# Mask products of a chunked recurrence: each head in its own row half of the array, without block diagonals

## The chip, the cores and the metric

The kernel runs on one core of a Trainium2 chip. The metric is the device time in microseconds (us). Two versions of the kernel are compared by the median of their runs; profiles are of one execution each. TensorE is the matrix engine, VectorE, ScalarE and GpSimd do the elementwise work, and SyncE issues most of the transfers. In the rows these are PE (matmuls) and PEld (TensorE's weight loads), DVE, ACT, POOL and SP.

## The reference, cut to what matters

The program is two layers on 256 tokens of width 2048, in fp32: the first of attention and a state space scan, the second of a short convolution and an RWKV-7 recurrence, each with its gated feed-forward part. The change lies in the recurrence of the second layer alone, which has 16 heads of 64 channels and runs over 16 meta tokens and then the 256 tokens:

```
def step(s, inp):                       # s: (heads, 64 values, 64 keys)
    r_t, w_t, k_t, v_t, a_t, b_t = inp
    sa = jnp.einsum('bhvk,bhk->bhv', s, a_t)
    s = s * w_t[:, :, None, :] + sa[..., None] * b_t[:, :, None, :] + v_t[..., None] * k_t[:, :, None, :]
    y_t = jnp.einsum('bhvk,bhk->bhv', s, r_t)
    return s, y_t
```

with a_t = -kk (the normalised key), b_t = kk times a rate, k_t another key, r_t the receptance and w_t a decay per channel.

## The kernel before, in words

The kernel does this step by chunks: one chunk of the 16 meta tokens (padded to 32) and four chunks of 64 tokens. Inside a chunk the dependence of each token on the earlier ones is written as masked products of decayed keys. For each head and chunk there are two of these mask products. The first multiplies the pair (b, k) with a; it is masked strictly and kept as AA (AAm for the meta chunk). The second multiplies the same pair (b, k) with r; it is masked with the diagonal and kept as RB. AA is solved by forward substitution on VectorE (`substitute`), and RB gives the outputs.

The channels lie on the 128 partitions, two heads to a block j: head e=0 on partitions 0 to 63, head e=1 on 64 to 127. There are eight blocks. The tile bk holds, for a block and a chunk, 64 columns of b and 64 of k; ar holds a and r; bkm and arm are their meta forms.

A matmul with bk as the stationary operand contracts over all 128 partitions, that is over both heads. To keep the heads apart, the kernel before writes the moving operand as a block diagonal: a tile with 64 columns for each head, filled with that head's a (or r) on its own 64 partitions and with zeros, set once, on the others. For AA these tiles are AD (two of them, by the parity of j) and ADm, filled by `spread` (L1032) with four ScalarE copies for each block. For RB it is RD (one tile for four blocks of a chunk), filled inside `products` (L1243) with two ScalarE copies. One call for a block and chunk then gives both heads: 128 columns of output, in 128 partitions (64 for b and 64 for k). Four such calls fill one PSUM bank, which VectorE multiplies with the mask into AA or RB.

`mixing(p2)` (L1038) makes AA for the blocks 2 p2 and 2 p2 + 1, all four chunks, and their meta product. `products(ci, g)` makes RB of chunk ci for four blocks. Both take their PSUM from `self.ps()`, the tag m, which has two banks; four banks belong to the gemms (`self.acc`) and two to the tag a. TensorE writes these in fp32; a call of `self.mm` (L99) with fp32 operands is two loads and two matmuls. The gemms take weights and activations as two parts, hi and lo, with three products for each.

What sets the order: while the gemms of the mixer run, `step()` after each gemm part (12 matmuls or so) calls the next piece of the recurrence, from a list of steps or from a list of due slots (`at(slot, f)`). `keys`, `key_norms` and `mixing` of the four pairs go in the gemms of the keys (`self.steps`), the last `mixing(3)` at slot 10 of the gemms after them, then `fetch`, which sends AA through DRAM to the layout of the substitution; the chunks with their `values`, `products`, `turn_keys`, `state_in`, `solve`, `state_out` and `outputs` go by slots later. The framework then orders the instructions of each engine by its own simulated times, with the program's order as the priority, and adds all semaphores. Each engine then runs its instructions in that fixed order.

Of the kernel before, what the change touches and what calls it, by code (L numbers as in the profile page):

```python
# [12 lines left out]
ALU = mybir.AluOpType  # L13
# [4 lines left out]
P = 128  # L18
# [24 lines left out]
class Net:  # L43
# [850 lines left out]
    def block2_mixer(self):  # L894
        nc, a = self.nc, self.a
        v = nc.vector
# [11 lines left out]
        ar = self.t(pp, [P, 8, 4, 2, 64], "ar")  # L908
        bk = self.t(pp, [P, 8, 4, 2, 64], "bk")
        arm = self.t(pp, [P, 8, 2, 32], "arm")  # L910
        bkm = self.t(pp, [P, 8, 2, 32], "bkm")
# [30 lines left out]
        avp = self.pool("avp", ctx=c1)  # L942
        AV = self.t(avp, [P, 8, TOK], "AV")
        ms64, ms32 = self.mask(avp, "ms64", 64, True), self.mask(avp, "ms32", 32, True)
# [15 lines left out]
        hs = [slice(0, 64), slice(64, 128)]  # L960
        flat2 = lambda ap: ap.rearrange("p b t -> p (b t)")
# [33 lines left out]
        def keys(p2):  # L995
            wk = wk_[0]
            for i in range(2):
                j = 2 * p2 + i
                av = AV[:, j, :]
                en = self.t(wk, [P, 17 + 4 * 65], "en")  # L1000
                enc = en[:, 17:].rearrange("p (c t) -> p c t", t=65)[:, :, 1:]
                nc.scalar.activation(en, EL[:, j, :], AF.Exp, scale=DECAY)
                nc.scalar.activation(EL[:, j, :], EL[:, j, :], AF.Exp, scale=-DECAY)
                k = kt.pop(j)
                rp = self.ps("a")
                for s, (o, n) in enumerate(SEG):
                    lt = nbs[p2][:n, s * 4 + 2 * i:s * 4 + 2 * i + 2, :].rearrange("p e k -> p (e k)")
                    self.tr(rp[:, o:o + n], lt)
                kk = self.t(wk, [P, TOK], "w", bufs=4)
                v.scalar_tensor_tensor(kk, k, self.vec("k_k_2", j), rp[:, :TOK], op0=ALU.mult, op1=ALU.mult)  # L1010
                b = self.t(wk, [P, TOK], "w", bufs=4)
                v.tensor_tensor(b, kk, av, op=ALU.mult)
                nc.scalar.activation(av, av, AF.Identity, scale=self.vec("k_a_2", j), bias=oka[:, j:j + 1])
                kp = KP[:, j, :]
                v.tensor_tensor(kp, av, k, op=ALU.mult)
                v.scalar_tensor_tensor(ar[:, j, :, 0, :], main(kk), -1.0, ELc[:, j, :, 0:64],
                                       op0=ALU.mult, op1=ALU.mult)
                v.scalar_tensor_tensor(arm[:, j, 0, 0:META], kk[:, 0:META], -1.0, EL[:, j, 0:META],
                                       op0=ALU.mult, op1=ALU.mult)
                for w, src in ((0, b), (1, kp)):  # L1020
                    v.tensor_tensor(bk[:, j, :, w, :], main(src), enc, op=ALU.mult)
                    v.tensor_tensor(bkm[:, j, w, 0:META], src[:, 0:META], en[:, 1:17], op=ALU.mult)
                spread(j)

        AD = [self.t(avp, [P, 4, 2, 64], f"AD{i}") for i in range(2)]
        ADm = self.t(avp, [P, 2, 2, 32], "ADm")
        for x in (*AD, ADm):
            nc.gpsimd.memset(x, 0.0)
        AAe = AA.rearrange("p c (e j) t -> p c e j t", e=2)
        AAme = AAm.rearrange("p (e j) t -> p j e t", e=2)  # L1030

        def spread(j):  # L1032

            for e in range(2):
                nc.scalar.copy(AD[j % 2][hs[e], :, e, :], ar[hs[e], j, :, 0, :])
                nc.scalar.copy(ADm[hs[e], j % 2, e, :], arm[hs[e], j, 0, :])

        def mixing(p2):  # L1038

            for i in range(2):  # L1040
                j = 2 * p2 + i
                ps = self.ps()
                for c in range(4):
                    self.mm(ps[:, c * P:(c + 1) * P], flat2(bk[:, j, c, :, :]), flat2(AD[i][:, c, :, :]))
                v.tensor_tensor(AAe[:, :, :, j, :], ps.rearrange("p (c e t) -> p c e t", c=4, t=64),
                                ms64.unsqueeze(1).unsqueeze(1).to_broadcast([P, 4, 2, 64]), op=ALU.mult)
            ps = self.ps()
            for i in range(2):
                self.mm(ps[:64, i * 64:(i + 1) * 64], flat2(bkm[:, 2 * p2 + i, :, :]), flat2(ADm[:, i, :, :]))
            v.tensor_tensor(AAme[:, 2 * p2:2 * p2 + 2], ps[:64, :P].rearrange("p (j e t) -> p j e t", j=2, t=32),  # L1050
                            ms32.unsqueeze(1).unsqueeze(1).to_broadcast([64, 2, 2, 32]), op=ALU.mult)

        ac = self.gemm(w_in, 0, KT, R0 + 3072, [96, 96], self.xs2, TOK)
        self.shifted(zp, twd, ac[0], 24, 96)
# [4 lines left out]
        for p2 in range(4):  # L1059
            ac = self.gemm(w_in, 0, KT, R0 + 1024 + p2 * 256, [P, P], self.xs2, TOK)  # L1060
            if not p2:
                cl.close()
                wk = wk_[0] = self.pool("rwk", bufs=2, ctx=c1)
            for i in range(2):
                j = 2 * p2 + i
                kt[j] = self.t(wk, [P, TOK], "k", bufs=4)
                self.shifted(zp, kt[j], ac[i], 8 + j)
            self.steps = [None, part(key_norms, p2), part(mixing, p2 - 1) if p2 else None, part(keys, p2)]
# [121 lines left out]
        st_ = {}  # L1190
# [6 lines left out]
        def chunk(ci):  # L1197
            k = Chunk()
            k.C = C = 32 if ci == 0 else 64
            k.n = META if ci == 0 else 64  # L1200
            c = k.c = ci - 1
            if ci == 0:
                k.bk = lambda j: flat2(bkm[:, j, :, :])
                k.ar = lambda j: flat2(arm[:, j, :, :])
                k.rr = lambda h, g: arm[h, 4 * g:4 * g + 4, 1, :]
                k.aa = lambda e, j: AAm[:, 8 * e + j, :]
                k.v = lambda j: V[:, j, 16:80]
                k.mi = mi32
            else:
                k.bk = lambda j: flat2(bk[:, j, c, :, :])  # L1210
                k.ar = lambda j: flat2(ar[:, j, c, :, :])
                k.rr = lambda h, g: ar[h, 4 * g:4 * g + 4, c, 1, :]
                k.aa = lambda e, j: AA[:, c, 8 * e + j, :]
                k.v = lambda j: V[:, j, c * 64:c * 64 + 128]
                k.mi = mi64
            return k

        ch = [chunk(ci) for ci in range(5)]

        def open_chunks():  # L1220
            c2.close()
            c5.close()
            cE.close()
            st_["cp"] = self.pool("cp", bufs=1, ctx=c3)
            st_["XQ"] = self.t(st_["cp"], [P, 8, 2, 64], "XQ")
            st_["SD"] = self.t(st_["cp"], [P, 8, 2, 64], "SD")
            st_["RD"] = self.t(st_["cp"], [P, 4, 2, 64], "RD")
            nc.gpsimd.memset(st_["SD"], 0.0)
            nc.gpsimd.memset(st_["RD"], 0.0)

        def values(ci):

# [10 lines left out]
        def products(ci, g):  # L1243

            k = ch[ci]
            C = k.C
            RD = st_["RD"]
            if not g:
                k.RB = self.t(st_["cp"], [2 * C, 8, 2, C], "RB")
            for e in range(2):  # L1250
                nc.scalar.copy(RD[hs[e], :, e, :C], k.rr(hs[e], g))
            ps = self.ps()
            for i in range(4):
                j = 4 * g + i
                rd = RD[:, i, :, :C]
                self.mm(ps[:2 * C, 2 * i * C:2 * (i + 1) * C], k.bk(j), flat2(rd) if C == 64 else rd)
            v.tensor_tensor(k.RB[:, 4 * g:4 * g + 4], ps[:2 * C, :8 * C].rearrange("p (j e t) -> p j e t", j=4, t=C),
                            k.mi.unsqueeze(1).unsqueeze(1).to_broadcast([2 * C, 4, 2, C]), op=ALU.mult)

        def turn_keys(ci):  # L1260

# [138 lines left out]
        ORDER = "v0 v1 v2 v3 b0 b1 r0 r1 r2 r3 g c0 h0 b2 c1 h1 b3 c2 h2 c3 h3"  # L1400
        at = self.at
        at(10, part(mixing, 3))
        at(10 + 2, fetch)
        s0, ds = 14, 4
# [10 lines left out]
        names = ORDER.split()  # L1415
        m0 = max(m0 + 6, 0, 8 * max(i + 1 for i, x in enumerate(names) if x[0] in 'vrg') + 2)
        at(m0, open_chunks)
        at(m0, part(values, 0))
        at(m0 + 1, part(products, 0, 0))
# [4 lines left out]
        for ci in range(5):  # L1424
            o = m0 + 3 + int(ci * dc)
            for x in seq.split():
                nm, off = x.split(':')
                f, d, last, args = dict(i=(state_in, 0, 5, 1), s=(solve, 0, 5, 1), v=(values, 1, 5, 0),
                                        t=(state_out, 0, 4, 1), y=(outputs, 0, 5, 0), p=(products, 1, 5, 1),
                                        k=(turn_keys, 1, 4, 0), r=(turn, 0, 5, 0))[nm[0]]  # L1430
# [17 lines left out]
        with ExitStack() as c4:  # L1448
# [63 lines left out]
            for m in LATE:  # L1512
                d = self.t(wk, [P, 258], "d")
                v.tensor_tensor(d, M[:, m, :], row, op=ALU.mult)
                h = self.H[:, m, 14:]
# [256 lines left out]
```

## Time and profile before

| | |
|---|---|
| median of 3 runs | 2443.42 us (2443.02 to 2444.26) |
| the profiled execution | 2443.2 us, of which the span from first to last instruction is 2441.4 us |
| TensorE, matmuls and loads | busy 99% and 96% |
| VectorE, ScalarE, GpSimd | busy 67%, 46%, 2% |
| granted TensorE clock, mean | 0.998 of full speed |
| HBM | 175 GB/s over the span |

Busy times are sums over the whole span, or over a stretch where one is named. Matmuls overlap one another, and the end of each is modelled, so a busy TensorE may still be slowed; the distance from the start of one weight load to the start of the next is the better measure of what an instruction costs. In a timeline, instructions that follow one another with the same line and tiles stand in one row with their number, and its duration is from the start of the first to the end of the last. Line 99 is the helper that records every matmul, line 104 every transpose, so groups are told apart by their tiles.

### The profile page before, as it was taken

To read this page: it belongs to the slowest core of one execution; us is meant where nothing else is said; L and a number is where in the kernel's file an instruction comes from. 1 tells how busy PE (TensorE), PEld (TensorE's weight loads), DVE (VectorE), ACT (ScalarE), POOL (GpSimd) and SP (SyncE) were. 2 spreads that over 40 slices of the span, in tenths; PEclk is the share of its full clock that TensorE was granted. 3 is DMA by queue.
4 is the path that set the end of the run, shared out by engine and by line. 5 is a ranking of instruction groups with operands and counts; after the bars stand their busy time and mean duration, and the time that the engine had idled before them with its cause. 6 is when DMAs were issued, how large, how long until landed. Compare 5 with 4: busy or idle time off the path is not lost.

```text
span 2441.4 us, 46809 instructions
## 1 busy us (share of the span) xinstructions
PE 2419.5 (99%) x19655; PEld 2347.5 (96%) x19655; DVE 1645.8 (67%) x2857; ACT 1131.4 (46%) x1574; POOL 59.4 (2%) x229
## 2 busy tenths in 40 slices
PE   9999999999999999999999999999999999999998
PEld 9999999999999999999999989999998999889986
DVE  7667666776676577567678956856865566556656
ACT  6545554443444344345664444454544444434443
POOL 3000000000000000000000000000000000000000
PEclk9999999999999999999999999999999999999999
DMA  7666446555655655656446551464555555555554
GB/s 226 178 186 164 155 156 200 181 185 182 198 183 174 197 190 173 197 183 209 148 138 190 167 148 53 139 210 155 192 190 189 184 181 188 190 188 181 185 190 138
DMA packets 402132, 431.09 MB, mean 177 GB/s; under 512 B 18849, under 2 KB 375780, under 8 KB 401456
## 3 DMA queue, kind: packets, MB, share of 16 engines
q1 hardware_dynamic: 386912, 413.41, 52.8%
q10 hardware_dynamic: 13184, 12.04, 1.7%
q0 software_dynamic: 1824, 2.64, 1.0%
q8 instruction: 154, 2.52, 0.4%
q14 instruction: 58, 0.48, 0.1%
HBM read 421.83 MB, written 6.23 MB: 175 GB/s over the span
## 4 chain that ended last, share of the span: by engine, by line
PE 97%; DVE 1%; issue 0%; DMA 0%; ACTq 0%; ACT 0%; SPq 0%; DVEq 0%
PE acc L99 89%; PE a L99 4%; PE m L99 3%; PE m L104 1%; PE a L104 1%; DVE lo L109 0%; DMA raw<-in_w_in_dram 0%; DVE sub L1106 0%; ACTq L1122 0%; DVE sub L1107 0%; ACT hi L108 0%; DVE F L1732 0%; DVE KP L1352 0%; DVE hx L1389 0%; DVE sub L1115 0%
## 5 line engine op out<-in xcount | busy, mean ns | idle before, releaser
L109 DVE TENSOR_TENSOR lo<-raw,hi 128x1024 fp32r<-128x1024 f32 (+1 forms) x780 | 951.2, 1220 | 627.1 <-ACT hi L108 620.4
L108 ACT CAST hi<-raw 128x1024 fp32r<-128x1024 f32 (+1 forms) x780 | 815.6, 1046 | 1130.7 <-PE acc L99 1044.5
L99 PE MATMUL acc<-Xh,lo 128*128 128x256 f32 (+3 forms) x4296 | 1214.9, 283 | 3.5 <-DVE lo L109 3.5
L99 PE MATMUL acc<-Xh,hi 128*128 128x256 f32 (+3 forms) x4296 | 1213.9, 283 | 4.6 <-ACT Xh L115 2.4
L99 PE MATMUL acc<-Xl,hi 128*128 128x256 f32 (+3 forms) x4296 | 1216.9, 284 | 0.5 <-DVE Xl L116 0.5
L99 PEld LDWEIGHTS acc<-Xh,lo 128*128 128x128 f32 x4296 | 811.7, 189 | 6.2 <-DVE lo L109 4.6
L99 PEld LDWEIGHTS acc<-Xh,hi 128*128 128x128 f32 x4296 | 810.7, 189 | 7.2 <-ACT Xh L115 2.6
L99 PEld LDWEIGHTS acc<-Xl,hi 128*128 128x128 f32 x4296 | 808.2, 188 | 2.5 <-DVE Xl L116 0.9
L99 PE MATMUL acc<-ghi,lo 128*128 128x256 f32 x704 | 196.7, 280 | 0.4 <-DVE lo L109 0.4
L99 PE MATMUL acc<-glo,hi 128*128 128x256 f32 x704 | 196.8, 280 | 0.0
L99 PE MATMUL acc<-ghi,hi 128*128 128x256 f32 x704 | 196.7, 280 | 0.0
L99 PEld LDWEIGHTS acc<-ghi,lo 128*128 128x128 f32 x704 | 132.2, 188 | 0.7 <-DVE lo L109 0.7
L99 PEld LDWEIGHTS acc<-glo,hi 128*128 128x128 f32 x704 | 132.4, 188 | 0.0
L99 PEld LDWEIGHTS acc<-ghi,hi 128*128 128x128 f32 x704 | 132.3, 188 | 0.0
L99 PE MATMUL acc<-lo,ghi 128*128 128x512 f32 (+1 forms) x326 | 128.3, 394 | 0.0
L99 PE MATMUL acc<-hi,glo 128*128 128x512 f32 (+1 forms) x326 | 128.2, 394 | 0.0
L99 PE MATMUL acc<-hi,ghi 128*128 128x512 f32 (+1 forms) x326 | 116.1, 394 | 0.0
L99 PEld LDWEIGHTS acc<-hi,glo 128*128 128x128 f32 x326 | 61.1, 188 | 14.9
L99 PEld LDWEIGHTS acc<-hi,ghi 128*128 128x128 f32 x326 | 61.3, 188 | 14.4
L99 PEld LDWEIGHTS acc<-lo,ghi 128*128 128x128 f32 x326 | 61.1, 187 | 14.6
L817 DVE SCALAR_TENSOR_TENSOR fc<-fu,vt,fc 128x256 f32<-128x256 f32 x176 | 73.4, 480 | 0.0
L99 PE MATMUL acc<-M2l,hi 128*128 128x258 f32 x256 | 72.4, 285 | 0.5 <-DVE M2l L109 0.5
(492 smaller groups left out, 2304.7 us busy)
## 6 DMA issues: line engine op xcount, KB each, us to landing
raw<-in_w_in_dram SPq DMA_DIRECT2D x90, 1024.0 KB, 5.4
raw<-in_w_up_dram SPq DMA_DIRECT2D x88, 1024.0 KB, 5.2
raw<-in_w_gate_up_dram SPq DMA_DIRECT2D x87, 1024.0 KB, 5.2
raw<-in_w_down_dram SPq DMA_DIRECT2D x76, 1024.0 KB, 5.2
raw<-in_w_out_dram SPq DMA_DIRECT2D x32, 1024.0 KB, 5.5
raw<-in_w_down_dram SPq DMA_DIRECT2D x24, 512.0 KB, 3.4
Hd<-H ACTq DMA_DIRECT2D x1, 2176.0 KB, 10.0
H<-Hd ACTq DMA_DIRECT2D x1, 2176.0 KB, 9.4
```

What stands on the lines that cost most here:

```text
L99: self.nc.tensor.matmul(out, lhsT, rhs, start=start, stop=stop, skip_group_check=True)
L104: self.nc.tensor.transpose(out, in_, self.ident[base:base + p, base:base + p])
L108: self.nc.scalar.copy(hi, src)
L109: self.nc.vector.tensor_sub(lo, src, hi.bitcast(F32))
L817: v.scalar_tensor_tensor(c, u[:, tp:tp + SEQ], self.vec(f"ffn_conv_w:{tp}", m), c, op0=ALU.mult, op1=ALU.add)
```

## The change

The block diagonals AD, ADm and RD, their clearing and their copies go. Each head multiplies with its own 64 partitions of bk and of ar alone (`h` in `hs` is 0:64 or 64:128), so that a call has 64 rows of contraction, 128 columns of bk (64 for the meta chunk) and the 64 (32) columns of one head. The two heads of a block write to two PSUM banks, `two[0]` and `two[1]`, and each bank is masked by one VectorE instruction. `mixing` now fills both banks with eight calls of each head (two blocks, four chunks) before it masks them; `products` with four calls of each head. The two heads' calls alternate.

```diff
-                spread(j)
-        AD = [self.t(avp, [P, 4, 2, 64], f"AD{i}") for i in range(2)]
-        ADm = self.t(avp, [P, 2, 2, 32], "ADm")
-        def spread(j):
-            for e in range(2):
-                nc.scalar.copy(AD[j % 2][hs[e], :, e, :], ar[hs[e], j, :, 0, :])
-                nc.scalar.copy(ADm[hs[e], j % 2, e, :], arm[hs[e], j, 0, :])
         def mixing(p2):
+            two = [self.ps() for _ in range(2)]
             for i in range(2):
                 j = 2 * p2 + i
-                ps = self.ps()
                 for c in range(4):
-                    self.mm(ps[:, c * P:(c + 1) * P], flat2(bk[:, j, c, :, :]), flat2(AD[i][:, c, :, :]))
-                v.tensor_tensor(AAe[:, :, :, j, :], ps.rearrange("p (c e t) -> p c e t", c=4, t=64),
+                    for e, h in enumerate(hs):
+                        self.mm(two[e][:, (c * 2 + i) * 64:(c * 2 + i + 1) * 64], flat2(bk[h, j, c, :, :]),
+                                ar[h, j, c, 0, :])
+            for e in range(2):
+                v.tensor_tensor(AAe[:, :, e, 2 * p2:2 * p2 + 2, :], two[e].rearrange("p (c i t) -> p c i t", c=4, t=64),
                                 ms64.unsqueeze(1).unsqueeze(1).to_broadcast([P, 4, 2, 64]), op=ALU.mult)
-            ps = self.ps()
+            two = [self.ps() for _ in range(2)]
             for i in range(2):
-                self.mm(ps[:64, i * 64:(i + 1) * 64], flat2(bkm[:, 2 * p2 + i, :, :]), flat2(ADm[:, i, :, :]))
-            v.tensor_tensor(AAme[:, 2 * p2:2 * p2 + 2], ps[:64, :P].rearrange("p (j e t) -> p j e t", j=2, t=32),
-                            ms32.unsqueeze(1).unsqueeze(1).to_broadcast([64, 2, 2, 32]), op=ALU.mult)
+                for e, h in enumerate(hs):
+                    self.mm(two[e][:64, i * 32:(i + 1) * 32], flat2(bkm[h, 2 * p2 + i, :, :]), arm[h, 2 * p2 + i, 0, :])
+            for e in range(2):
+                v.tensor_tensor(AAme[:, 2 * p2:2 * p2 + 2, e, :], two[e][:64, :64].rearrange("p (j t) -> p j t", t=32),
+                                ms32.unsqueeze(1).to_broadcast([64, 2, 32]), op=ALU.mult)
...
-            st_["RD"] = self.t(st_["cp"], [P, 4, 2, 64], "RD")
-            nc.gpsimd.memset(st_["RD"], 0.0)
...
         def products(ci, g):
+            two = [self.ps() for _ in range(2)]
+            for i in range(4):
+                for e, h in enumerate(hs):
+                    self.mm(two[e][:2 * C, i * C:(i + 1) * C], k.bk(4 * g + i, h), k.rr(h, 4 * g + i))
             for e in range(2):
-                nc.scalar.copy(RD[hs[e], :, e, :C], k.rr(hs[e], g))
-            ps = self.ps()
-            for i in range(4):
-                j = 4 * g + i
-                rd = RD[:, i, :, :C]
-                self.mm(ps[:2 * C, 2 * i * C:2 * (i + 1) * C], k.bk(j), flat2(rd) if C == 64 else rd)
-            v.tensor_tensor(k.RB[:, 4 * g:4 * g + 4], ps[:2 * C, :8 * C].rearrange("p (j e t) -> p j e t", j=4, t=C),
-                            k.mi.unsqueeze(1).unsqueeze(1).to_broadcast([2 * C, 4, 2, C]), op=ALU.mult)
+                v.tensor_tensor(k.RB[:, 4 * g:4 * g + 4, e], two[e][:2 * C, :4 * C].rearrange("p (j t) -> p j t", t=C),
+                                k.mi.unsqueeze(1).to_broadcast([2 * C, 4, C]), op=ALU.mult)
```

## Rows read from the trace of the kernel before

**Rows 1.** The page, part 1: busy us (share of the span) xinstructions, by engine.
```profile
PE 2419.5 (99%) x19655; PEld 2347.5 (96%) x19655; DVE 1645.8 (67%) x2857; ACT 1131.4 (46%) x1574; POOL 59.4 (2%) x229
```

**Rows 2.** The page, part 4: the chain that ended last, by engine.
```profile
PE 97%; DVE 1%; issue 0%; DMA 0%; ACTq 0%; ACT 0%; SPq 0%; DVEq 0%
```

**Rows 3.** Two stretches: busy us (instructions) of PE, PEld, DVE, ACT, POOL; clock, DMA.
```profile
1215.00:1300.00 85.00, 85.00 (x682) 82.52 (x682) 66.21 (x173) 50.80 (x96) 2.59 (x16) 1.00 0.48 145
...
1440.00:1550.00 110.00, 110.00 (x1209) 101.69 (x1207) 74.62 (x169) 54.96 (x90) 6.03 (x7) 1.00 0.23 68
```

**Rows 4.** The tile AD: duration in ns min/median/max, first and last start.
```profile
L99 PEld LDWEIGHTS m<-AD,bk x64: 186/192/193, 1222.5 to 1293.6; 128*128 128x128 f32 x64
...
L1035 ACT COPY AD<-ar x16: 388/402/404, 1218.5 to 1285.6; 64x256 f32<-64x256 f32 x16
```

**Rows 5.** The tile ADm, the same columns.
```profile
L1036 ACT COPY ADm<-arm x16: 214/216/221, 1219.3 to 1286.2; 64x32 f32<-64x32 f32 x16
L99 PEld LDWEIGHTS m<-ADm,bkm x16: 133/138/139, 1229.4 to 1295.0; 128*64 128x64 f32 x16
```

**Rows 6.** The tile RD, the same columns.
```profile
L99 PEld LDWEIGHTS m<-RD,bk x64: 186/192/193, 1459.5 to 1535.8; 128*128 128x128 f32 x64
...
L99 PEld LDWEIGHTS m<-RD,bkm x16: 132/138/139, 1446.2 to 1449.1; 128*64 128x64 f32 x16
...
L1251 ACT COPY RD<-ar x16: 401/404/407, 1449.5 to 1530.4; 64x256 f32<-64x256 f32 x16
L1251 ACT COPY RD<-arm x4: 295/297/299, 1442.3 to 1447.3; 64x128 f32<-64x128 f32 x4
```

**Rows 7.** Timeline of weight loads: start, us, form, number; a burst on RD.
```profile
1459.35 0.19 PEld L99 LDWEIGHTS acc<-Xh,lo 128*128 128x128 f32 x1
1459.47 0.97 PEld L99 LDWEIGHTS m<-RD,bk 128*128 128x128 f32 x8
1460.37 0.19 PEld L99 LDWEIGHTS acc<-Xh,hi 128*128 128x128 f32 x1
```

**Rows 8.** The same timeline: a burst of 64 rows by 64 columns.
```profile
1468.99 0.19 PEld L99 LDWEIGHTS acc<-Xh,hi 128*128 128x128 f32 x1
1469.32 1.94 PEld L99 LDWEIGHTS a<-XQ,AA 64*64 64x64 f32 x32
1471.32 0.19 PEld L99 LDWEIGHTS acc<-Xl,hi 128*128 128x128 f32 x1
```

**Rows 9.** The same timeline: state products, the heads in alternating column halves.
```profile
1461.41 0.54 PEld L99 LDWEIGHTS m<-UV,BT 64*64 64x64 f32 x16
1462.02 0.97 PEld L99 LDWEIGHTS a<-SD,ar 128*128 128x128 f32 x8
```

**Rows 10.** Weight loads of transposes, 1440 to 1550 us: busy us, mean ns of one.
```profile
L104 PEld LDWEIGHTS m<-ident,V 128*128 128x128 f32 x32 | 3.4, 141 | 0.4
...
L104 PEld LDWEIGHTS m<-ident,yc 64*128 64x128 f32 x24 | 1.7, 138 | 0.3
```

**Rows 11.** Timeline of weight loads: an RD burst and the burst before it.
```profile
1463.11 0.19 PEld L99 LDWEIGHTS a<-UV,AA 128*64 128x64 f32 x2
1463.37 0.97 PEld L99 LDWEIGHTS m<-RD,bk 128*128 128x128 f32 x8
```

**Rows 12.** Timeline of weight loads: the first AD burst and what follows it.
```profile
1222.55 0.31 PEld L99 LDWEIGHTS m<-AD,bk 128*128 128x128 f32 x2
...
1222.78 1.32 PEld L99 LDWEIGHTS a<-bd,w 128*128 128x128 f32 x12
```

**Rows 13.** The tiles AA and RB: VectorE's mask instructions, ns min/median/max.
```profile
L1045 DVE TENSOR_TENSOR AA<-m,ms x8: 668/672/692, 1226.0 to 1295.0; 128x512 f32<-128x512 f32 x8
...
L1257 DVE TENSOR_TENSOR RB<-m,mi x10: 415/692/692, 1446.9 to 1536.2; 128x512 f32<-128x512 f32 x8, 64x256 f32<-64x256 f32 x2
```

**Rows 14.** TensorE's waits, 1385 to 1420 us: us in total, times, longest.
```profile
PE acc L99 <- ACT hi L108: 2.2, 1, 2.2
PE acc L99 <- DVE lo L109: 1.9, 3, 0.8
```

More of the change, by code (lines that the diff above doesn't have):

```diff
@@ L1022, in keys @@
                     v.tensor_tensor(bkm[:, j, w, 0:META], src[:, 0:META], en[:, 1:17], op=ALU.mult)
-                spread(j)
-        AD = [self.t(avp, [P, 4, 2, 64], f"AD{i}") for i in range(2)]
-        ADm = self.t(avp, [P, 2, 2, 32], "ADm")
-        for x in (*AD, ADm):
-            nc.gpsimd.memset(x, 0.0)
         AAe = AA.rearrange("p c (e j) t -> p c e j t", e=2)
         AAme = AAm.rearrange("p (e j) t -> p j e t", e=2)
-        def spread(j):
-            for e in range(2):
-                nc.scalar.copy(AD[j % 2][hs[e], :, e, :], ar[hs[e], j, :, 0, :])
-                nc.scalar.copy(ADm[hs[e], j % 2, e, :], arm[hs[e], j, 0, :])
@@ L1202, in chunk @@
             if ci == 0:
-                k.bk = lambda j: flat2(bkm[:, j, :, :])
+                k.bk = lambda j, h=slice(0, P): flat2(bkm[h, j, :, :])
                 k.ar = lambda j: flat2(arm[:, j, :, :])
-                k.rr = lambda h, g: arm[h, 4 * g:4 * g + 4, 1, :]
+                k.rr = lambda h, j: arm[h, j, 1, :]
                 k.aa = lambda e, j: AAm[:, 8 * e + j, :]
@@ L1209, in chunk @@
             else:
-                k.bk = lambda j: flat2(bk[:, j, c, :, :])
+                k.bk = lambda j, h=slice(0, P): flat2(bk[h, j, c, :, :])
                 k.ar = lambda j: flat2(ar[:, j, c, :, :])
-                k.rr = lambda h, g: ar[h, 4 * g:4 * g + 4, c, 1, :]
+                k.rr = lambda h, j: ar[h, j, c, 1, :]
                 k.aa = lambda e, j: AA[:, c, 8 * e + j, :]
@@ L1246, in products @@
             C = k.C
-            RD = st_["RD"]
             if not g:
                 k.RB = self.t(st_["cp"], [2 * C, 8, 2, C], "RB")
+            two = [self.ps() for _ in range(2)]
+            for i in range(4):
+                for e, h in enumerate(hs):
+                    self.mm(two[e][:2 * C, i * C:(i + 1) * C], k.bk(4 * g + i, h), k.rr(h, 4 * g + i))
             for e in range(2):
-                nc.scalar.copy(RD[hs[e], :, e, :C], k.rr(hs[e], g))
-            ps = self.ps()
-            for i in range(4):
-                j = 4 * g + i
-                rd = RD[:, i, :, :C]
-                self.mm(ps[:2 * C, 2 * i * C:2 * (i + 1) * C], k.bk(j), flat2(rd) if C == 64 else rd)
-            v.tensor_tensor(k.RB[:, 4 * g:4 * g + 4], ps[:2 * C, :8 * C].rearrange("p (j e t) -> p j e t", j=4, t=C),
-                            k.mi.unsqueeze(1).unsqueeze(1).to_broadcast([2 * C, 4, 2, C]), op=ALU.mult)
+                v.tensor_tensor(k.RB[:, 4 * g:4 * g + 4, e], two[e][:2 * C, :4 * C].rearrange("p (j t) -> p j t", t=C),
+                                k.mi.unsqueeze(1).to_broadcast([2 * C, 4, C]), op=ALU.mult)
         def turn_keys(ci):
```

## The prediction

> **What bounds the kernel now.** I read first the busy shares of the page, then the chain of waits, then the busy time of the engines by stretch. TensorE is busy for 2419.5 of 2441.4 us, with as many weight loads as matmuls [rows 1], and the chain that ended last lies on it for 97% [rows 2]. In the two stretches that the change touches, the mask products of A (1215 to 1300 us) and the recurrence (1440 to 1550 us), it is busy without a gap, while VectorE and ScalarE have room [rows 3]. So time taken off ScalarE is worth nothing here by itself, and what TensorE needs more or less for the changed products goes to the end one for one: behind each of them stands a gemm whose matmuls are ready. Within TensorE I go by the starts of the weight loads, since a matmul's end is modelled: from one load to the next is what an instruction costs.
>
> **What an instruction costs today.** An fp32 multiply is two loads and two matmuls: 32 calls on AD gave 64 of each [rows 4]. In a burst of eight on RD the loads stand (0.97 - 0.191) / 7 = 0.111 us apart; it begins 0.12 us after a gemm's load, the gemm's own step, and the next gemm load comes 8 x 0.111 = 0.89 us on [rows 6, 7]. Such a burst, the full 128 rows of the array, thus costs its loads and nothing for going in and out. A burst that uses part of the array is different. The 32 loads of 64 rows by 64 columns stand (1.94 - 0.135) / 31 = 0.058 us apart; the burst begins 0.33 us after the last gemm load, 0.21 more than the step, and its 32 x 0.058 = 1.86 us end at 1471.18, 0.14 us before the next gemm load [rows 8]. So going in and out costs 0.35 us for each burst.
>
> **The change, part by part.**
>
> *Loads of the main products.* Each of the 64 calls on block diagonals (32 for A, 32 for the four chunks) becomes two: half the rows, all 128 columns of keys, 64 moving columns instead of 128. That makes 256 loads out of 128 [rows 4, 6]. A load of half the rows is not shorter: among the transposes of the recurrence 64 rows by 128 columns last 138 ns, 128 by 128 last 141 [rows 10]. The trace has no row halves that alternate, so their step is bounded. Above: 0.111 us each, one behind the other. Below: two at a time, 0.056 us. The nearest rows are the products that alternate column halves, written head by head as the new ones are: 16 loads of 64 by 64 stand (0.54 - 0.135) / 15 = 0.027 us apart [rows 9], under half of the 0.058 of the same size on one place [rows 8]. Halves of the array thus load side by side here, if they are column halves. I take this for the row halves as well: 256 x 0.056 = 14.2 us against 128 x 0.111 = 14.2 us, a term of 0. The upper end is +14.2 us.
>
> The Trainium skill says of weight loads (TensorE: Matmul & The Clock Gate, LDWEIGHTS) that the time goes by the columns and not by the rows; this speaks against the change, and the 138 beside 141 ns agree. By it alone the main loads would take 28.4 us, 14.2 more. It also says (TensorEngine Tiling (Array Packing), Key Properties) that different tiles load and multiply in parallel, and that a change of tiling mode drains the engine; with that the 14.2 us go away again. The trace shows the first for column halves, and the second as the 0.35 us of a burst.
>
> *Loads of the meta products.* 32 loads become 64 [rows 5, 6], of 64 columns: side by side 64 x 0.027 = 1.7 us, before 32 x 0.057 = 1.8 us: 0. One behind the other they cost 1.9 us more. These bursts used part of the array before, so their way in and out is paid already.
>
> *Ways in and out.* The main bursts now pay them. A's products are four bursts, one for each pair of key blocks: 4 x 0.35 = 1.4 us. Of the eight RD bursts three stand between gemm work on both sides (3 x 0.35 = 1.05), three have one neighbour that uses part of the array already (some 0.17 each, 0.5), and two have such neighbours on both sides and paid before, like that at 1463.37 between two bursts of 64 columns [rows 11]. Sum 2.95, so +3.0 us. If the program's scheduler cuts the bursts of A in two (two of the four pairs are cut today by the key norms, as at 1222.78 [rows 12]), 4 x 0.35 = 1.4 come on top; if all stand beside other such bursts, all falls to 0.
>
> *The copies.* 32 copies for A and 20 for the chunks go: 16 x 0.402 + 16 x 0.216 + 16 x 0.404 + 4 x 0.297 = 17.5 us of ScalarE [rows 4 to 6]. TensorE, busy throughout [rows 3], covers them; taken as 0. Nothing is late next in their place: the products wait for the decayed keys, as before.
>
> *Masks on VectorE.* A's two evictions of a pair keep their size (0.672 us [rows 13]); each RB one of 0.692 us becomes two of half the columns, for which the shortest RB row stands, 0.415 us at that number of columns [rows 13]. That is about 0.14 us more for each of eight, 1.1 us in all, with some 0.1 us more for each of the six meta ones: under 2 us, on an engine that is idle for 35 us of the recurrence's 110 [rows 3]. Hidden.
>
> *Banks.* A pair now fills both banks of the tag m at once, and its meta products need both back; before, they needed one, and it was read while the second block was multiplied. Behind a TensorE that waits there stands all gemm work. The scheduler can put gemm matmuls between, as it puts other products between the parts of a pair today [rows 12], so 0. The upper end is two evictions in the open, 2 x 0.68 = 1.36 us for each of four pairs, and 2 x 0.42 = 0.84 for those of eight products where the next user of m follows at once: 5 to 8 us.
>
> Sum: 0 + 0 + 3.0 + 0 = +3.0 us on the profiled execution's own 2443.2 us (span 2441.4 and 1.8 around it), which lies 0.2 us under the median of 2443.42: **2446.3 us**, +0.1%. A measurement of this kernel can tell some 0.2%, 4.9 us, from no change, so this is no change, a little on the slow side. The likeliest case's own range is 2443 to 2449.
>
> **Rivals.**
> 1. *The row halves load one behind the other.* For it: no pair of row halves is in the trace, and the columns loaded double. Against: the column halves [rows 9]. Price: 14.2 + 1.9 + 3.0 = 19 us, 2462 us. It decides as soon as the step within a new burst is nearer 0.111 than 0.056 us: past 0.068 us the whole change is over 4.9 us. Slower.
> 2. *TensorE waits for its banks.* For it: both banks go at once and two evictions stand behind the last matmul. Against: the gemm work that can be put between. Price 5 to 8 us over the forecast: 2451 us at 5. Slower.
> 3. *It gets faster.* The last AD copies hold back the mask products that the substitution starts from, and in that stage TensorE does wait, 2.2 us for ScalarE and 1.9 for VectorE [rows 14]. Were all of that saved and all bursts placed beside others (0 for the ways in and out), the time would be 2443.2 - 4.1 = 2439 us. Against: these waits come 90 us later, and the substitution is placed by counting gemm parts, not by when A is ready.
> 4. *The heads still share an array pass or a bank, so the change doesn't do what it says.* The operands start at rows 0 and 64 and go to two tiles, so I see no way; no chance of its own.
>
> **How the numbers follow.** The forecast gets 0.60, rival 1 0.20, rival 2 0.12, rival 3 0.08. In the forecast's case 0.85 falls within 0.2%, 0.13 above and 0.02 below; rival 1 is all above; rival 2 is above in nine of ten; rival 3 is half within, half below. Faster: 0.01 + 0.04 + some for what I don't see, 0.07. Slower: 0.08 + 0.20 + 0.11, rounded down to 0.37. Same: 0.56. The range takes in rival 3 without its end, all of rival 2, and rival 1 up to its middle: 2440 to 2463 us.
>
> **What would show it.** In the weight loads of a new burst: a mean step of 0.056 us (128 columns) and 0.027 to 0.03 (64) for the forecast, 0.111 and 0.058 for rival 1. The first load of a burst 0.33 us after a gemm's, the next gemm load 0.14 us late. TensorE without a gap in both stretches, else rival 2. The prediction is wrong if the step is not halved, if A's bursts come in many pieces, or if time moves in a stretch without changed products.

## The result and the profile after

The changed kernel takes 2459.55 us (2458.41 to 2459.84, 4 runs) beside 2443.22 us (2442.39 to 2444.26, 4 runs) of the kernel before, measured beside it: +16.3 us, a ratio of 1.0060 [1.0048, 1.0073]. It is slower, by more than the 0.2% that a measurement of this kernel can tell. The forecast, 2446.3 us, was the sum of +3.0 us; 13 us came on top, inside the range, but outside the likeliest case.

The page of the changed kernel, busy shares of the engines and the chain by engine:

```profile
PE 2436.4 (99%) x19815; PEld 2359.4 (96%) x19815; DVE 1649.1 (67%) x2871; ACT 1114.9 (45%) x1522; POOL 57.7 (2%) x225
...
PE 91%; DVE 4%; DMA 1%; issue 1%; ACTq 0%; ACT 0%; POOL 0%; DVEq 0%; POOLq 0%
```

Beside [rows 1], TensorE has 160 more loads, as counted (128 main, 32 meta), and is busy 17 us longer. ScalarE lost 16.5 us of its 1131.4 (forecast 17.5), and nothing came of it. VectorE gained 3.3. TensorE's share of the chain fell from 97% [rows 2] to 91% because the chain now runs over A's masks, their transfer and the substitution on VectorE from 1282 to 1406 us; TensorE itself waits for only 4.9 us there, as the waits below show.

The two stretches of [rows 3], of the changed kernel (busy us and instructions of PE, PEld, DVE, ACT, POOL; clock; DMA):

```profile
1215.00:1300.00 85.00, 82.72 (x703) 78.37 (x703) 63.88 (x179) 39.38 (x61) 2.59 (x16) 0.98 0.52 142
1440.00:1550.00 110.00, 110.00 (x1127) 99.37 (x1125) 72.20 (x167) 41.44 (x60) 2.84 (x3) 1.00 0.19 59
```

In the recurrence TensorE is still busy without a gap, and yet does 82 matmuls less in the 110 us: it doesn't wait, so its instructions cost more (in part these are others, as the program has shifted by some microseconds; the same work is compared further down). The first stretch has a gap of 2.3 us, which is two waits near 1295 us. Its waits from 1200 to 1300 us, and then from 1385 to 1420 us (us in total, times, longest):

```profile
PE acc L99 <- ACT hi L108: 1.8, 1, 1.8
PE acc L99 <- DVE lo L109: 0.5, 1, 0.5
```

```profile
PE acc L99 <- ACT hi L108: 1.4, 1, 1.4
PE acc L99 <- DVE lo L109: 1.2, 2, 0.8
```

The kernel before had no wait in the first of them and 4.1 us in the second [rows 14]; now it is 2.3 and 2.6. Waiting moved forward and grew from 4.1 to 4.9 us: it explains less than 1 us.

Now the loads themselves. The tiles bk and bkm with ar and arm, which answer to [rows 4 to 6], and the mask instructions, which answer to [rows 13] (ns min/median/max, first and last start):

```profile
L99 PEld LDWEIGHTS m<-ar,bk x256: 182/188/188, 1223.2 to 1537.2; 64*128 64x128 f32 x128
...
L99 PEld LDWEIGHTS m<-arm,bkm x64: 129/135/135, 1231.0 to 1437.0; 64*64 64x64 f32 x64
...
L1037 DVE TENSOR_TENSOR AA<-m,ms x8: 679/682/693, 1228.2 to 1282.5; 128x512 f32<-128x512 f32 x8
...
L1246 DVE TENSOR_TENSOR RB<-m,mi x20: 273/424/426, 1433.9 to 1537.5; 128x256 f32<-128x256 f32 x16, 64x128 f32<-64x128 f32 x4
```

Twice the loads, each as long as before (188 and 192 ns by their records): a row half is no shorter. Whether two go at once is seen only in the distances of their starts. Two timelines of weight loads of the changed kernel (start, us, form, number). First a burst of A:

```profile
1226.44 0.19 PEld L99 LDWEIGHTS acc<-Xh,hi 128*128 128x128 f32 x1
1226.78 0.97 PEld L99 LDWEIGHTS m<-ar,bk 64*128 64x128 f32 x16
1227.82 0.19 PEld L99 LDWEIGHTS acc<-Xl,hi 128*128 128x128 f32 x1
```

and then one of a chunk:

```profile
1447.73 0.54 PEld L99 LDWEIGHTS m<-UV,BT 64*64 64x64 f32 x16
1448.34 0.96 PEld L99 LDWEIGHTS m<-ar,bk 64*128 64x128 f32 x8
1449.37 0.19 PEld L99 LDWEIGHTS acc<-Xh,lo 128*128 128x128 f32 x1
```

Sixteen loads in 0.97 us, and eight in 0.96. The single starts, in us from 1226.7 and from 1448.3, show why:

```
A:     0.081 0.088  0.189 0.196  0.299 0.305  0.410 0.417  0.522 0.529  0.634 0.640  0.745 0.752  0.857 0.864
chunk: 0.040        0.148        0.257        0.369        0.481        0.592        0.704        0.816
```

In A's burst the loads come in pairs, one of each head, 0.007 us apart, and a pair every 0.111 us: 0.056 for a load, as forecast. The chunk's burst holds the eight loads of one head alone, 0.111 us apart. (The records don't name the head of a load; I read it from the steps and the order of the program.) All 128 loads of A's main products are paired (64 pairs); of the 128 of the chunks' main products none is. The framework's scheduler issued all four calls of one head and, later, all four of the other, in 14 of the 15 bursts; in the fifteenth the two stand one behind the other.

To see where the time went I cut both traces at the same two gemm loads (the 9681st and the 11841st of their kind) and summed the distances from each weight load's start to the next one's. Of a step longer than 0.45 us, all beyond a gemm load's usual 0.12 us is counted as a wait.

| us | window | changed loads (number, bursts) | gemm loads | other loads | waits |
|---|---|---|---|---|---|
| before | 376.8 | 17.7 (160, 24) | 269.4 | 83.8 | 6.1 |
| after | 393.5 | 28.2 (320, 31) | 273.3 | 85.7 | 6.3 |

The window is 16.7 us longer, the whole of the result. Of it 10.5 are steps of the changed loads: the chunks' main ones went from 7.7 to 16.0, A's from 7.2 to 8.0, the meta ones from 2.7 to 4.2 (three of A's four meta bursts were cut in two, one head in each, and two of the chunks' three hold one head alone: these 40 loads stand 0.058 us apart, the other 24 in pairs, 0.029 per load). The rest, 5.8 beside the waits, lies in the steps of the neighbours: ways in and out of more bursts, and 3.4 us more at half clock, which I haven't parted.

### The profile page after: what moved, and what is told of

The parts are those of the page before. It is cut to its first block, busy times and chain, and to the rows that moved or that the text cites. A ratio compares the mean times of both kernels' runs of the same rounds, so it can differ in the third digit from the quotient of the medians.

```text
span 2458.0 us, 47083 instructions
## 1 busy us (share of the span) xinstructions
PE 2436.4 (99%) x19815; PEld 2359.4 (96%) x19815; DVE 1649.1 (67%) x2871; ACT 1114.9 (45%) x1522; POOL 57.7 (2%) x225
## 4 chain that ended last, share of the span: by engine, by line
PE 91%; DVE 4%; DMA 1%; issue 1%; ACTq 0%; ACT 0%; POOL 0%; DVEq 0%; POOLq 0%
PE acc L99 83%; PE a L99 4%; PE m L99 3%; DVE lo L109 1%; DVE sub L1100 1%; PE m L104 1%; DVE sub L1101 0%; PE a L104 0%; DMA BC<-rd 0%; DMA AAd<-AA 0%; ACT hi L108 0%; ACTq L1116 0%; DMA Zd<-sub 0%; DVE r L882 0%; ACTq L1090 0%
## 5 line engine op out<-in xcount | busy, mean ns | idle before, releaser
L99 PE MATMUL acc<-M2h,hi 128*128 128x258 f32 x256 | 73.3, 289 | 0.0
```

Of the source, the lines that this page charges most:

```text
L99: self.nc.tensor.matmul(out, lhsT, rhs, start=start, stop=stop, skip_group_check=True)
```

## The experiments

Two theories. *Order*: the forecast's sum holds for heads that alternate, and the loss is that the scheduler, given two banks that come free at different times, put the chunks' heads one behind the other. *Rival*: row halves are dear in themselves (the number of bursts, ways in and out, the lower granted clock), whatever the order.

Since the granted clock differs from run to run, the table gives a second figure: the mean over a kernel's runs of time times mean granted clock, less the same for the kernel before on that chip (2437.3 to 2438.6 us). It counts each microsecond at half clock as half a one. That is right where TensorE works at that clock and takes off too much where it waits, and the falls of the clock can themselves be an effect of the change, so it is an aid and no second measurement; the clock of a run is given to 0.001, so it is good to about 1 us. For the changed kernel the clocks of its own runs of before are not on record, hence its range.

| kernel | median us (runs) | ratio to before | difference, us | at full clock | mean clock | changed loads, us (bursts) |
|---|---|---|---|---|---|---|
| after | 2459.55 (4) | 1.0060 [1.0048, 1.0073] | +16.3 | +13 to +15 | 0.9970 | 28.2 (31) |
| e1_mix_only | 2446.25 (11) | 1.0009 [1.0000, 1.0018] | +2.2 | +1.7 | 0.9970 | 19.0 (23) |
| e2_prod_only | 2460.19 (5) | 1.0068 [1.0056, 1.0081] | +16.1 | +11.2 | 0.9950 | 26.7 (32) |
| e3_held | 2447.91 (11) | 1.0016 [1.0007, 1.0024] | +3.8 | +4.3 | 0.9975 | 19.4 (22) |
| e10_held_again | 2446.77 (11) | 1.0011 [1.0002, 1.0020] | +1.9 | +4.0 | 0.9975 | 19.4 (22) |
| e9_both_in_turn | 2455.24 (6) | 1.0048 [1.0035, 1.0060] | +10.4 | +9.0 | 0.9958 | 23.5 (21) |
| e3_chain | 2459.93 (5) | 1.0060 [1.0048, 1.0073] | +14.0 | +9.7 | 0.9950 | 22.9 (34) |
| e4_prod_held | 2457.10 (5) | 1.0046 [1.0033, 1.0058] | +11.2 | +7.1 | 0.9954 | 18.6 (25) |
| e8_held_in_turn | 2457.58 (5) | 1.0045 [1.0032, 1.0057] | +11.6 | +6.3 | 0.9952 | 22.6 (24) |
| e5_heads_in_turn | 2473.85 (4) | 1.0119 [1.0106, 1.0133] | +29.8 | +21.8 | 0.9942 | 33.1 (33) |
| e6_acc_banks | 2473.16 (4) | 1.0112 [1.0097, 1.0128] | +27.2 | +9.8 | 0.9900 | 22.4 (27) |

None of the ten medians fell where the theory expected it, and by the median alone the rival's condition was met in e4_prod_held, e8_held_in_turn and e6_acc_banks. The argument therefore rests on the starts of the loads, on the sums of their steps, and on e9_both_in_turn beside e10_held_again, which differ in the order alone and ran on one chip.

**Each half alone.** e1_mix_only has the new `mixing` and the old `products`; e2_prod_only the other way round.

> The change in A's mask products alone; the chunks' products as before. Theory (row halves load side by side when the two heads' calls alternate; the chunks' products lost this because the scheduler issued all of one head, then all of the other): A's main bursts step 0.056 us and lose only the ways in and out, six bursts x 0.35 = 2.1 us, and three more meta bursts with theirs, 1.5 us; with waits around the fetch of A, 4 to 8 us slower than before (2447 to 2451). Rival (row halves cost TensorE twice the load time wherever they are used): about half of the 16 us and more, 8 to 10 us slower.

> The change in the chunks' products alone; A's mask products as before. Theory: the heads come one after the other, 16 bursts of 8 loads at 0.112 us, 8.3 us more in steps and 2 to 3 in ways in and out: 9 to 12 us slower than before (2452 to 2455). Rival (twice the load time everywhere): 8 us slower; the two then differ in the bursts' steps rather than in this time.

A's half costs +2.2 us, the chunks' half +16.1. At full clock it is 1.7 and 11.2, whose sum, 12.9, is about what the whole change shows: the parts add up, and the loss sits in the chunks. e1 came in below what both theories said (4 to 8 and 8 to 10 us). e2's median missed its 9 to 12 us; its changed loads grew by 9.0 us, and at full clock it is 11.2 over. The rest is the granted clock, 0.9950, on which more at the end.

**The order held.** e3_held is the changed kernel with each burst tied together: after the first call of a burst every call must follow the one written before it. The first of the two banks is claimed by a VectorE instruction, and the chain begins with the second, so that a burst starts only when both are free.

```diff
         def products(ci, g):
             two = [self.ps() for _ in range(2)]
-            for i in range(4):
-                for e, h in enumerate(hs):
-                    self.mm(two[e][:2 * C, i * C:(i + 1) * C], k.bk(4 * g + i, h), k.rr(h, 4 * g + i))
+            v.memset(two[0][:, 0:1], 0.0)
+            self.chain([(two[e][:2 * C, i * C:(i + 1) * C], k.bk(4 * g + i, hs[e]), k.rr(hs[e], 4 * g + i))
+                        for i in range(4) for e in (1, 0)])
```

and in `mixing` the same for the meta products; A's main products, which were paired already, are only chained, from the first bank on and without a claim.

> The changed kernel with the two heads' calls held in alternation: the first bank is claimed by a one-column clear on VectorE, and the calls of a burst are queued one behind the other, beginning with the second bank. Theory: the chunks' bursts become one of 16 loads at 0.056 us each, so 18.1 us (steps, ways in and out) become 10.2; A's meta bursts become one each, 1.6 us less: 2449 to 2452 us, 5 to 9 us over before. Rival (the order of the heads doesn't matter): 2457 to 2461 us, as the changed kernel.

Measured +3.8 us, and +1.9 as e10_held_again on another chip, both below the 5 to 9 and the 3 to 5 expected: the forecast's own sum, +3.0, lies between. 62 of at most 64 pairs of the chunks' loads are back, the steps are 19.4 us beside 17.7 before the change, and the bursts are 22. So the changed products, with the same calls, banks and masks and a few one-column clears more, cost about what was forecast once they are issued in the order in which they are written; some 12 us of the 16 (9 to 11 at full clock) are the order in which the scheduler issued them, pairing and number of bursts together.

**Order or number of bursts.** Holding gave both an alternation and fewer bursts. To part them, e9_both_in_turn is e3_held with `for e in (1, 0) for i in range(4)` in the chunks' chain: one burst, the heads one behind the other. e10_held_again is e3_held on the same chip.

> As e3_held (A and the chunks, each burst held together), but within a burst of the chunks one head's four calls come before the other's; A's bursts alternate as before. Theory (what the changed kernel loses is the order of the heads): the chunks' loads stand some 0.09 us apart instead of 0.06, as in e8_held_in_turn, about +4 us of steps over e3_held, bursts as many as there; the time 4 us over e3_held, about 2452 us, and the 16 loads of a burst take 1.5 us, not 1.0. Rival (the loss is the number of bursts and their ways in and out, not the order): within 1 us of e3_held, about 2448 us.

> The kernel of e3_held once more, on the same chip as e9_both_in_turn, so that the two are compared with each other. Both theories: 3 to 5 us over the kernel before, as e3_held (+3.8).

A chunk's burst in e10_held_again and in e9_both_in_turn, timelines of weight loads:

```profile
1452.69 0.19 PEld L99 LDWEIGHTS acc<-Xh,hi 128*128 128x128 f32 x1
1453.02 0.97 PEld L99 LDWEIGHTS m<-ar,bk 64*128 64x128 f32 x16
1454.05 0.97 PEld L99 LDWEIGHTS a<-SD,ar 128*128 128x128 f32 x8
```

```profile
1475.79 0.19 PEld L99 LDWEIGHTS acc<-Xh,hi 128*128 128x128 f32 x1
1476.11 1.47 PEld L99 LDWEIGHTS m<-ar,bk 64*128 64x128 f32 x16
1477.64 0.97 PEld L99 LDWEIGHTS a<-SD,ar 128*128 128x128 f32 x8
```

The same sixteen loads take 0.97 us or 1.47 by the order alone, with as many bursts (22 and 21). The steps differ by 4.1 us (about +4 expected), the time at full clock by 5.0, the median by 8.5; the intervals of the two ratios don't touch. The order within a burst is shown to cost 4 to 5 us, though the median moved by more than that. The 9 bursts more that the changed kernel has against e3_held come from heads in separate bursts, with loads beside which none of the other head runs (28.2 us against 23.5) and more ways in and out; this part of the loss is read from the sums of the steps and not tested by itself.

**The chain alone.** e3_chain ties the calls as e3_held does, but claims no bank, and begins with the first one.

> As the changed kernel with both products held, but the second bank is not claimed beforehand: the calls are queued in alternation, and the first of each burst goes as soon as one bank is free, alone, the rest later. 13 bursts more, of one call each. Theory (a burst costs 0.35 us for its way in and out, a call by itself 0.06 us for a step that is not shared): 4.5 to 6 us more than with both held, 2452 to 2454 us. Rival (ways in and out cost nothing of their own): within 1.5 us of it.

Outside A's main products the first call of 13 of the 14 bursts now goes off alone, and other work is put before the rest, as it would if only the first bank were free then. Weight loads of e3_chain:

```profile
1543.47 0.29 PEld L99 LDWEIGHTS m<-ar,bk 64*128 64x128 f32 x2
1543.83 0.19 PEld L99 LDWEIGHTS a<-XQ,AA 64*64 64x64 f32 x2
1544.08 0.19 PEld L99 LDWEIGHTS acc<-Xh,lo 128*128 128x128 f32 x1
1544.19 0.19 PEld L99 LDWEIGHTS acc<-Xh,hi 128*128 128x128 f32 x1
1544.52 0.96 PEld L99 LDWEIGHTS m<-ar,bk 64*128 64x128 f32 x14
```

That makes 34 bursts, not 22, and the time at full clock is 5.4 us over e3_held, where 4.5 to 6 was expected. But 1.7 us of it are waits (9.0 us beside 7.3), so that the twelve more ways in and out, with the loads that go unpaired in them, come to less than was expected. The median is 12 over it, a miss: the clock fell too (0.9950).

**Heads in turn in A.** e5_heads_in_turn is the changed kernel with A's loops turned, all of head 0 and then all of head 1 (`for e, h in enumerate(hs)` outermost). A's pairs, which the scheduler had kept, go.

> The changed kernel with the loops of A's main products turned: all calls of head 0, then all of head 1, so that they do not alternate. Same instructions, same banks. Theory: A's 128 loads step 0.112 instead of 0.056 us, 7 us on top of the changed kernel: 2465 to 2468 us. Rival (the order of the heads doesn't matter): 2458 to 2461 us.

Timeline of weight loads, a burst of A in e5_heads_in_turn:

```profile
1229.13 0.19 PEld L99 LDWEIGHTS acc<-Xh,hi 128*128 128x128 f32 x1
1229.46 1.46 PEld L99 LDWEIGHTS m<-ar,bk 64*128 64x128 f32 x16
1231.00 0.19 PEld L99 LDWEIGHTS acc<-Xl,hi 128*128 128x128 f32 x1
```

1.46 us for what took 0.97 in the changed kernel. That is 0.085 us for a load, not the 0.112 expected: two heads in turn within one burst overlap in part (more at the end). So the steps grew by 4.9 us and not by 7. The time at full clock is 7 to 9 us over the changed kernel, but only by luck near the +7 expected, as the waits grew by 5 us (11.3 beside 6.3). The median is 14 over it, outside its range, and there the clock comes in as well (0.9942).

**The chunks alone, held.** e4_prod_held is e2_prod_only with the chunks held as in e3_held; e8_held_in_turn is e4 with the heads in turn.

> The chunks' products alone changed, with the two heads' calls held in alternation in one burst; A's mask products as before. Theory: load steps as before the change, only ways in and out added; with both products held the kernel is 3.8 us over before and with A's alone 2.2 us, so this one 1 to 3 us over before (2445 to 2447). Rival (two heads' products of the chunks cost more for another reason, such as their evictions or banks): 8 us or more over before.

> As the kernel with the chunks' products alone held, with the same banks, the same claim and the same bursts, but within a burst all calls of one head, then all of the other. Theory: 128 main loads step 0.112 instead of 0.056 us and 32 meta loads 0.058 instead of 0.029, 8 us more than that kernel (2453 to 2456), and more where the granted clock falls. Rival (it was the number of bursts and their ways that cost, not the order of the heads): within 1.5 us of that kernel.

e4's steps did what was expected (18.6 us, 0.9 over the kernel before; e2 had 26.7), and 5 us of e2's loss went. But its time missed: +11.2. TensorE's waits of e4_prod_held, 1540 to 1620 us:

```profile
PE m L113 <- DVE yc L1341: 4.6, 1, 4.6
PE acc L99 <- ACT M2h L117: 1.0, 1, 1.0
PE acc L99 <- DVE M2l L118: 0.2, 1, 0.2
```

The last chunk ends after the gemms that cover it, and TensorE waits 4.6 us for it; the kernel before waits 0.5 there and e10_held_again 0.8. The clock is at half for 6.8 us after that wait. e8 has 4 us more in its steps and 4 us less of waits, and so the same time, 0.5 us more where 8 were expected: by the time the rival's condition (within 1.5 us) is met, and only the steps speak for the order. Why the same chunks end late with the old `mixing` ahead of them and not with the new stays open; their schedules differ ahead of the chunks already.

**Other banks.** e6_acc_banks takes the chunks' two banks from the four of the gemms (`two = [self.acc() for _ in range(2)]`), with nothing held.

> The changed kernel with nothing held, but the chunks' products take their two PSUM banks from the gemms' four instead of the two of the tag m. Theory (the heads were taken apart because the two banks of the tag m come free at different times): the scheduler now leaves most of the calls in alternation by itself, half or more of the chunks' loads come 0.007 us after the other head's, and the time lies between the held and the changed kernel, 2448 to 2455 us, unless the gemms wait for their banks. Rival (the scheduler takes the heads apart for another reason, such as the order of their operands): runs of 8 loads of one head as in the changed kernel, 2457 us or more.

A chunk's burst in e6_acc_banks, its waits from 1380 to 1430 us, and the window around them:

```profile
1439.69 0.19 PEld L99 LDWEIGHTS acc<-Xh,lo 128*128 128x128 f32 x1
1440.01 0.97 PEld L99 LDWEIGHTS acc<-ar,bk 64*128 64x128 f32 x16
1441.05 0.19 PEld L99 LDWEIGHTS acc<-Xh,hi 128*128 128x128 f32 x1
```

```profile
PE m L99 <- DMA sub<-Td: 11.7, 1, 11.7
PE acc L99 <- DVE gc L1369: 4.0, 2, 3.3
```

```profile
1394.00:1424.00 30.00, 17.60 (x283) 17.29 (x283) 3.66 (x8) 5.18 (x9) 2.72 (x3) 0.50 0.43 89
```

With other banks and no tie 48 of the 64 pairs are back, as the theory had it. So which banks the products take decides how the scheduler orders them. The time missed its range: it was lost ahead of the chunks, to 15.7 us of waits, 11.7 for the transfer of the substitution's result and 4.0 for VectorE's gc, which reads banks of the gemms, with the clock at half around them. That the cause is the different times at which the two banks of tag m come free is argued from this and from e3_held, not shown by itself.

## Why the prediction was right or wrong

- *Loads of the main products* (0, bounded by +14.2). The mechanism holds: row halves load side by side, 0.056 us each, and the rule drawn from column halves [rows 9] carried over. It was 24.0 us beside 14.9, though, because half of the loads had no partner. The Trainium skill says (TensorEngine Tiling (Array Packing), Key Properties) that different tiles can load and multiply in parallel; A's bursts agree, at 0.056 us, and the chunks', at 0.111, show that tiles issued in separate bursts don't.
- *Banks* is the step that failed: "The scheduler can put gemm matmuls between, as it puts other products between the parts of a pair today, so 0." It did that, and TensorE never waited for a bank in the chunks. But what was put between stood between the two heads, and the pairing of the term above was lost with it: 16.0 us instead of 7.7 for the chunks' steps, and 31 bursts instead of 24. I had costed two terms by themselves that exclude each other: either the bursts are held and TensorE may wait, or they are split and the loads don't pair. The price of rival 1 came about for the chunks' half, in the place that rival 2 named; neither rival had this mechanism, and rival 1's test, the step in a new burst, gave 0.056 in A and 0.111 in the chunks. So it is luck that the time lies inside the range: the range reached that far for rival 1, which did not occur as it was told. By the prediction's own signs (a step that is not halved, A's bursts in many pieces) it was wrong for the chunks and for the meta products.
- *Loads of the meta products* (0): 4.2 us beside 2.7. The step in an undivided burst is right (0.029 per load). But 40 of the 64 loads stand in bursts of one head, 0.058 apart, so that this term lost its pairing as the main one did, and the divided bursts pay a way in and out each.
- *Ways in and out* (+3.0): right in size, 0.34 us in and 0.15 beyond the last step at 1226.78, 0.33 and 0.14 forecast. The number of bursts was wrong for the chunks. With the order held the total was +3.8 and +1.9.
- *Copies* (0) and *masks* (hidden): right. The masks of RB came to 0.424 us (0.415 taken); VectorE's 3.3 us more in all, where under 2 were forecast, stay hidden.
- *Rival 3*: the waits it named went from 4.1 to 2.6 us, but 2.3 us of others came up near 1295 us, so that nothing was gained.
- One figure of rival 1 is mis-worked: the step past which the whole change is over 4.9 us is 0.056 + (4.9 - 3.0) / 256 = 0.063 us, not 0.068. Nothing hangs on it, as the steps came out at 0.056 and 0.111.

## What to carry to other kernels

In these runs array tiles ran fully side by side only as neighbours in the order in which the engine issues them, and writing them so in the program is not enough where a scheduler may move them: tie the calls, and claim both outputs before the first. A cost of zero "because the scheduler puts other work there" has to be checked against every other term that needs the work to stay together. And where removed work was off the path (17 us of ScalarE here), no more than a version that does as well was to be expected: none of those run here beat the kernel before.

## What the runs showed of the hardware that was not expected

Two heads written one behind the other in one burst do overlap, in part. The 16 starts of the burst at 1476.11 us in e9_both_in_turn, in us from 1476.0:

```
0.110 0.218 0.327 0.439  0.551 0.611 0.662 0.719 0.774 0.828 0.886 0.940  1.052 1.163 1.275 1.387
```

Four loads go alone, 0.11 us apart, then eight at 0.055, then four alone. As I read it, after half of the first head's loads the second head's begin beside the rest, so that in this burst a load found a partner a few loads ahead, but not a whole burst ahead.

And the granted clock fell where TensorE waited for nothing. In e5_heads_in_turn no wait is recorded from 1200 to 1300 us; its first burst of row halves in turn begins at 1223.86 us, and the clock goes to the lower level (1.2 GHz) at 1225.2, for 3.4 us, as it does behind the third burst, at 1245.7. Windows of that kernel:

```profile
1215.00:1225.00 10.00, 10.00 (x86) 9.54 (x84) 9.81 (x28) 6.18 (x13) 0.19 (x2) 1.00 0.55 179
1225.00:1229.00 4.00, 4.00 (x21) 3.89 (x20) 1.43 (x8) 0.86 (x2) 0.01 (x1) 0.57 0.22 71
1229.00:1245.00 16.00, 16.00 (x135) 14.94 (x134) 12.52 (x34) 8.56 (x15) 0.10 (x1) 1.00 0.40 122
```

The gemm steps behind that burst are 0.23 us, not 0.12. In e9_both_in_turn it is the same at 1510.2 us, behind such a burst and 16 loads of 64 by 64, with no wait from 1500 to 1517 us:

```profile
1500.00:1510.00 10.00, 10.00 (x118) 9.22 (x115) 9.38 (x25) 2.27 (x4) 0.94 (x1) 1.00 0.36 105
1510.00:1517.00 7.00, 7.00 (x45) 6.20 (x43) 0.06 (x1) 2.06 (x4) 0.00 (x0) 0.51 0.01 2
```

The longest such fall was in e2_prod_only, 17 us from 1448.6, behind meta products in row halves and other small products, with no wait from 1420 to 1470 us:

```profile
1425.00:1445.00 20.00, 20.00 (x311) 19.42 (x308) 7.34 (x11) 10.41 (x15) 2.73 (x3) 1.00 0.39 120
...
1450.00:1460.00 10.00, 10.00 (x63) 7.93 (x63) 1.51 (x2) 4.31 (x7) 0.00 (x0) 0.50 0.05 7
```

Where this happens, an unpaired half of the array is paid for twice, in its own steps and in the steps of what follows. That such bursts bring the fall about is not shown: behind all of the chunks' unpaired bursts of the changed kernel, 1430 to 1540 us, the clock stayed at the upper level. In the kernel before the one fall of the clock in this part, at 1418.2 us, stands behind TensorE's waits [rows 14]. How often the clock falls differs from run to run of one kernel (0.993 to 0.998 in e9_both_in_turn, 2452 to 2462 us), and the times here move with it.
